# Reordering the stretch between the dense part and the experts, ending on a small pair, and summing the last tiles half in PSUM and half on VectorE

## The chip, the core and the metric

The kernel runs on one core of a Trainium2 chip. The metric is device time in microseconds (us). The engines are TensorE (PE: matmuls; PEld: its weight loads), VectorE (DVE), ScalarE (ACT), GpSimd (POOL) and SyncE (SP), which here only issues DMAs. Each engine takes its instructions in its own program order and waits on semaphores for the others. SBUF holds tiles of 128 partitions; PSUM holds what TensorE accumulates.

## What is computed

One layer of a decoder trunk over 1024 tokens of width 1024, in float32, and a final RMSNorm. Its dense part is a conditioned norm, one combined projection, a convolution branch and an mLSTM branch, and an output projection. Behind it stands a mixture of 32 experts: each token chooses one group of four and in it two of eight experts.

```python
x = x + gt1[:, None, :] * y                      # dense part
h = modulate(rmsnorm(x, g_norm2[l]), sh2, sc2)
g_sel = argmax(softmax(h @ w_rg + b_rg))         # one group of 4
top_p, top_e = top_k(softmax((h @ w_re + b_re)[group]), 2)
w_tok = p_g * top_p / sum(top_p)
y = sum over the 2 experts e of w_tok[e] * ((silu(h @ w_e_gate[e]) * (h @ w_e_up[e])) @ w_e_down[e])
x = x + gt2[:, None, :] * y
return rmsnorm(x, g_final)
```

Each expert has 3 x 2 MB of weights; all 32 are read, 192 MB.

## The kernel before, in words

Tokens lie in 8 tiles of 128 (`NT = 8`; `LT`, the last, is tile 7). The dense part ends with the output product of each tile (`products`, six or so matmuls to a k of eight), its residual (`residual`, DVE), its second norm, its router logits (`router_T` transposes, `router`) and the choice of experts (`choose`, DVE, some thirty small operations; `weigh` computes the softmax weights, in steps that the queue `fill`/`drain` hands out between other work). Tile 7 is done in two halves, so that its choice ends last. Then ranks are counted (`ranks_early`, `set_key`), and one order of experts by load is made (`places`: `elist`, `capr`, `pos`).

After that the experts run as *blocks* of 128 slots. Blocks 0 to 15 have one expert each; their weights are split on the chip into two fp32r parts, `wh` (a cast on ACT) and `wl` (a subtraction on DVE), and multiplied in three passes. Block 0's up and down weights are taken whole, in fp32 (`WHOLE`). Blocks 16 to 23 (`SMALL`) are pairs of experts with 64 slots each and take their weights as they are. Block 24 (`TWB`) shares the weights of block 2. A block goes through `st_sel` (a 0/1 matrix from positions, DVE 128x2048), `st_slots` (16 small matmuls give the slots' token numbers and weights, DVE turns them into indices, POOL gathers the rows `xg` from `h_d`), `st_x` (transpose), `st_gu` (gate and up products), `st_act`, `st_h` and `st_down` (product with the down weights; `ye` is the weighted result, scattered by POOL into `y_d`).

The table `units` sets the order of blocks and with it the order of the weight stream: 192 DMAs of 1 MB on SP into six buffers `big`, each issued when its buffer has been used up. A block's up and gate weights are asked for ahead of the down weights of the one before it. Four of the six buffers exist only once the dense part's memory is released (`yp.release()`, line 1550).

The last `LATE` blocks (two before) are not scattered. Their results are split in high and low parts (`yh`, `yl`) and put to the tokens by matmuls with the transposed 0/1 matrix (`selT`). The rest is read back: 16 loads `y_d` of 512 KB, queued on SP behind the weights (`load_y`), two for each token tile. For tiles 0 and 1 these are added to the residual `mg` by POOL or DVE, for tiles 2 to 7 one of the two is added to the other by POOL and the sum then to `mg` by DVE (tiles 2, 3) or, for tiles 4 to 7, by matmuls with the identity into the same PSUM. Then `final_norm` (ACT square with a sum, two small POOL operations) and `final_out` (DVE, then a DMA).

```python
units = [[0], [1], [16], [2, TWB], [17], [3], [4], [18], [5], [6], [19], [7], [8], [20], [9], [10], [21], [11], [12],
         [22], [13], [23], [14], [15]]
```

Of the kernel before, what the change touches and what calls it, by code (L numbers as in the profile page):

```python
# [8 lines left out]
F32 = mybir.dt.float32  # L9
# [27 lines left out]
LATE = 2  # L37
# [5 lines left out]
def hybrid_layer_kernel(ctx: ExitStack, tc: tile.TileContext, x, c, w_ada, b_ada, g_norm1, w_in, b_if,  # L43
# [1164 lines left out]
    rev = rp.tile([P, EPG], F32, name="rev")  # L1208
    t4 = [rp.tile([P, NT, NG], F32, name=f"t4{i}") for i in range(3)]
# [126 lines left out]
    def order_of_experts():  # L1336
# [17 lines left out]
        ts(tw[0:NE], ion[0:NE], rc, OP.is_equal)  # L1354
        yield 0
# [12 lines left out]
        kp = mo.tile([P, NT, NE], F32, tag="tHL", bufs=2, name="kp")  # L1368
        ts(kp, rank, float(P), OP.is_ge, float(P * (TWB - FIX - 1)), OP.mult)
        tt(kp, kp, rank, OP.add)  # L1370
# [79 lines left out]
    def add_pieces(b, wi):  # L1450
        for q in range(2):
            for r in places(b):
# [8 lines left out]
             [22], [13], [23], [14], [15]]  # L1461
# [14 lines left out]
    for t in range(NT):  # L1476
# [18 lines left out]
        if t < NT - 1:  # L1495
            for k in range(KT):
                products(k, (0, 1))
                if k == 2 and t > 0:
                    router_T(t - 1)
# [10 lines left out]
            for _ in range(6 if t < 6 else 20):  # L1510
                fill(0)
# [37 lines left out]
    sel_into(0, slice(0, LT))  # L1549
# [84 lines left out]

    identb = rp.tile([P, P], BF16, name="identb")
    V.tensor_copy(identb, ident)
# [114 lines left out]
    def st_down(unit):  # L1751
# [24 lines left out]
        for b in unit:  # L1776
# [4 lines left out]
            for hf in range(2):  # L1781
                sl = slice(hf * 512, (hf + 1) * 512)
                stt(y[:, sl], py[b][hf], d["wsl"], gt2[:, sl], OP.mult, OP.mult)
                if b == blocks[-1]:
                    split(yhl[0][:, sl], yhl[1][:, sl], y[:, sl])
            if late:
                lates.append(yhl + [y])
# [4 lines left out]
    for r in range(FIX):  # L1792
        if r:
            sel_into(r, slice(0, LT))
# [46 lines left out]
    def load_y():  # L1841

        W.room()
        bufs = [W.buffers()[i // 2][:, i % 2 * D:(i % 2 + 1) * D] for i in range(9)]
        bufs += [xgs[(len(blocks) + i) % 3] for i in range(3)]
# [225 lines left out]
```

## Time and profile before

| | |
|---|---|
| median of 3 runs | 1435.85 us (1435.72 to 1435.99) |
| the profiled execution: its own time | 1434.2 us |
| its span, from first to last instruction | 1432.4 us |
| mean granted TensorE clock | 0.963 |
| busy: PE, DVE, ACT, POOL | 1303.9, 999.9, 513.7, 326.8 us |

Four stretches are seen in the page's forty slices: the dense part to about 796 us, in which TensorE is busy; the boundary, about 796 to 870 us, in which TensorE and the DMA engines both have gaps; the stream of expert weights, whose last byte lies about 1390 us; and the end to 1432 us, with the sums and the last norm. A busy TensorE has its engine's share near 1; a full DMA system has a share near 1.0 at about 400 GB/s.

### The profile page before, as it was taken

To read this page: it belongs to the slowest core of one execution; us is meant where nothing else is said; L and a number is where in the kernel's file an instruction comes from. 1 tells how busy PE (TensorE), PEld (TensorE's weight loads), DVE (VectorE), ACT (ScalarE), POOL (GpSimd) and SP (SyncE) were. 2 spreads that over 40 slices of the span, in tenths; PEclk is the share of its full clock that TensorE was granted. 3 is DMA by queue.
4 is the path that set the end of the run, shared out by engine and by line. 5 is a ranking of instruction groups with operands and counts; after the bars stand their busy time and mean duration, and the time that the engine had idled before them with its cause. 6 is when DMAs were issued, how large, how long until landed. Compare 5 with 4: busy or idle time off the path is not lost. (4 is left out here: it accounts for less than half of the span.)

```text
span 1432.4 us, 17703 instructions
## 1 busy us (share of the span) xinstructions
PE 1303.9 (91%) x6627; PEld 973.3 (68%) x6627; DVE 999.9 (70%) x1371; ACT 513.7 (36%) x682; POOL 326.8 (23%) x265
## 2 busy tenths in 40 slices
PE   4799989999989999999999679999899999999976
PEld 3687888879878888777887445656465565654554
DVE  6979998889976761655556685457676675754587
ACT  5233143333532224411222323335344353533442
POOL 3333455231331310115222010001111111110033
PEclk9799989999999999999999899999999999999998
DMA  9433443333353433444521578899999999999982
GB/s 288 126 118 133 140 140 119 132 118 88 115 175 125 154 114 129 168 155 154 175 102 59 191 259 331 331 379 407 418 414 404 407 401 402 405 385 399 397 337 119
DMA packets 121161, 337.13 MB, mean 235 GB/s; under 512 B 12481, under 2 KB 74221, under 8 KB 96240
## 3 DMA queue, kind: packets, MB, share of 16 engines
q1 hardware_dynamic: 106064, 290.81, 54.4%
q0 software_dynamic: 14528, 43.56, 8.1%
q10 hardware_dynamic: 480, 1.59, 0.3%
q8 instruction: 53, 0.87, 0.2%
q14 instruction: 36, 0.29, 0.1%
HBM read 303.37 MB, written 41.45 MB: 241 GB/s over the span
## 5 line engine op out<-in xcount | busy, mean ns | idle before, releaser
L56 DVE TENSOR_TENSOR wl<-big,wh 128x1024 fp32r<-128x1024 f32 x184 | 224.7, 1256 | 104.5 <-ACT wh L148 103.4
L148 ACT CAST wh<-big 128x1024 fp32r<-128x1024 f32 x184 | 185.5, 1048 | 174.8 <-DMA big<-in_w_e_gate_dram 90.8
L64 DVE SCALAR_TENSOR_TENSOR cacc<-u,vec,cacc 128x1024 f32<-128x1024 f32 x120 | 212.0, 1767 | 2.9
L67 PE MATMUL z<-hH,wh 128*128 128x512 f32 x512 | 166.3, 407 | 7.4 <-DVE hH L377 5.1
L67 PE MATMUL gu<-wh,tHLx 128*128 128x512 f32 x528 | 169.3, 401 | 2.6 <-ACT wh L148 2.6
L67 PE MATMUL z<-hL,wh 128*128 128x512 f32 x512 | 163.0, 400 | 1.4 <-DVE hL L56 1.2
L67 PE MATMUL z<-hH,wl 128*128 128x512 f32 x512 | 162.2, 398 | 0.0
L67 PE MATMUL gu<-big,tFx 128*64 128x512 f32 (+1 forms) x528 | 131.8, 628 | 0.0
L67 PEld LDWEIGHTS gu<-wh,tHLx 128*128 128x128 f32 x528 | 96.7, 189 | 29.5 <-ACT wh L148 9.5
L67 PEld LDWEIGHTS z<-hH,wh 128*128 128x128 f32 x512 | 96.2, 192 | 29.3 <-ACT hH L380 5.1
L67 PEld LDWEIGHTS z<-hL,wh 128*128 128x128 f32 x512 | 97.3, 190 | 26.1 <-DVE hL L56 1.9
L67 PEld LDWEIGHTS z<-hH,wl 128*128 128x128 f32 x512 | 97.3, 190 | 23.6 <-DVE wl L56 0.2
L67 PE MATMUL gu<-wl,tHLx 128*128 128x512 f32 x264 | 106.1, 402 | 7.7 <-DVE wl L56 7.6
L1617 POOL DMA_INDIRECT y_d<-ye,idx x23 | 32.6, 1416 | 339.1 <-DVE ye L64 319.0
L56 DVE TENSOR_TENSOR wl<-raw,wh 128x1024 fp32r<-128x1024 f32 (+1 forms) x45 | 70.7, 1575 | 39.5 <-ACT wh L148 39.5
L67 PEld LDWEIGHTS gu<-big,tFx 128*64 128x64 f32 (+1 forms) x528 | 39.8, 146 | 73.7 <-issue 71.6
L56 POOL TENSOR_TENSOR acc<-acc,ar 128x1024 f32<-128x1024 f32 x24 | 70.5, 2939 | 61.5 <-ACT ar L572 51.8
L67 PE MATMUL zt<-wl,hH 128*128 128x256 f32 (+1 forms) x256 | 76.1, 297 | 4.5 <-DVE wl L56 4.5
L67 PE MATMUL zt<-wh,hH 128*128 128x256 f32 (+1 forms) x256 | 77.3, 302 | 0.8 <-ACT qk L659 0.7
L67 PE MATMUL zt<-wh,hL 128*128 128x256 f32 (+1 forms) x256 | 76.2, 298 | 0.0
L67 PE MATMUL o<-woH,mHL 128*128 128x512 f32 x256 | 72.9, 401 | 0.0
L67 PE MATMUL py<-wh,tHLh 128*128 128x512 f32 x256 | 72.5, 405 | 0.1
(403 smaller groups left out, 2193.2 us busy)
## 6 DMA issues: line engine op xcount, KB each, us to landing
big<-in_w_e_gate_dram SPq DMA_DIRECT2D x64, 1024.0 KB
big<-in_w_e_up_dram SPq DMA_DIRECT2D x64, 1024.0 KB
big<-in_w_e_down_dram SPq DMA_DIRECT2D x64, 1024.0 KB
raw<-in_w_in_dram SPq DMA_DIRECT2D x38, 512.0 KB
ar<-in_w_ada_dram SPq DMA_DIRECT2D x16, 1024.0 KB
araw<-in_w_ada_dram SPq DMA_DIRECT2D x8, 1024.0 KB
y_d<-zero SPq DMA_DIRECT2D x16, 512.0 KB
big<-y_d SPq DMA_DIRECT2D x9, 512.0 KB
```

What stands on the lines that cost most here:

```text
L56: return eng.tensor_tensor(out=o, in0=a, in1=b, op=op)
L64: return V.scalar_tensor_tensor(out=o, in0=a, scalar=s, in1=b, op0=op0, op1=op1)
L67: return PE.matmul(o, l, r, start=start, stop=stop)
L148: S.copy(h, src)
L1617: G.indirect_dma_start(out=y_d[:, :], out_offset=bass.IndirectOffsetOnAxis(ap=idx[:, 1:2], axis=0), in_=src, in_offset=None, bounds_check= ...
```

## The change

In the boundary: the weights of the choice (`drain`) are finished inside tile 6, the router of tiles 6 and 7 is put at other steps of the product, both 0/1 matrices for tokens of tiles 0 to 6 are made together, the constant `identb` is made earlier, a one-element Silu is put ahead of block 0, one weight piece is split ahead of its transposed rows, the third `xg` is cleared later, block 16's slots come behind all four up steps of block 0, and block 0's own slots behind those; block 17's slots and the overflow counts come later in the loop.

At the end: the unit order, `LATE` one instead of two (so block 14 is now scattered as well, and only block 23 is put in by `selT`), `selT` made one unit earlier, the loads of `y_d` in the order of `ENDS` into other buffers, and the sums: tiles 0 to 3 take the residual and both loads into PSUM by identity matmuls and are normed from there, tiles 4 to 7 take both loads on DVE.

```diff
-LATE = 2
+LATE = 1
+    V.tensor_copy(identb, ident)          # moved up from before by_slot
+        ts(kp, rank, float(P), OP.is_ge, float(P * (TWB - FIX - 1)), OP.mult)   # moved up in places()
+        tt(kp, kp, rank, OP.add)
-             [22], [13], [23], [14], [15]]
+             [22], [13], [14], [15], [23]]
+                if k == 1 and t == NT - 2:
+                    drain()
-            for _ in range(6 if t < 6 else 20):
+            for _ in range(6):
                 fill(0)
...
-                if k == 3:
+                if k == 2:
                     router_T(t - 1)
-            router(t - 1)
+                if k == 5:
+                    router(t - 1)
...
-                if k == KT - 1:
-                    router(t, (0,))
                 products(k, (1,))
-                if k == 3:
+                if k == 4:
                     router_T(t, (0,))
-                if k == 5:
+                if k == 6:
                     ranks_early()
...
+            router(t, (0,))
-    sel_into(0, slice(0, LT))
+    for r in range(FIX):
+        sel_into(r, slice(0, LT))
...
-    for g_ in xgs:
+    def clear_xg(g_):
         S.activation(k3(g_), iota.unsqueeze(1).broadcast_to([P, KT, P]), AF.Copy, scale=0.0)
+    for g_ in xgs[0:2]:
+        clear_xg(g_)
...
                 stt(y[:, sl], py[b][hf], d["wsl"], gt2[:, sl], OP.mult, OP.mult)
-                if b == blocks[-1]:
+                if late:
                     split(yhl[0][:, sl], yhl[1][:, sl], y[:, sl])
...
+    S.activation(mo.tile([P, 1], F32, tag="silu", bufs=1, name="silu"), pio, AF.Silu)
+    W.split()
+    clear_xg(xgs[2])
     next(places_)
     st_x(0)
-    W.split()
-    W.split()
+    next(places_)
     next(rest)
-    next(places_)
     for _ in rest:
         pass
     W.nsplit = 4
-    st_gu(0, 0, 0, 4)
     for b in blocks_of(2):
         st_sel(b)
+    st_gu(0, 0, 0, 4)
+    W.split()
     W.split()
     W.split()
     st_x(1)
-    st_gu(0, 1, 0, 2)
+    st_sel(0)
+    st_gu(0, 1, 0, 4)
     for b in blocks_of(2):
         st_slots(b)
-    st_sel(0)
-    st_gu(0, 1, 2, 4)
     st_slots(0, False)
...
+        bufs = list(xgs)                  # load_y: 3 xg, 4 whl, 4 u, 4 halves of big, 1 tHL
...
+        for t in ENDS:
             for i in range(2):
-                yin[t, i] = bufs[2 * t + i]
+                yin[t, i] = bufs.pop(0)
                 nc.sync.dma_start(yin[t, i], y_d[i * T + t * P:i * T + (t + 1) * P, :])
+    ENDS = (4, 0, 5, 1, 6, 2, 7, 3)
+    def by_ident(t, a, start):
+        for hf in range(2):
+            mm(ends[t][hf], ident, a[hf], start, False)
+    def begin_end(t):
+        ends[t] = zps.tile([P, 2, 512], F32, tag="z", name=f"yl{t}")
+        ends[t] = [ends[t][:, 0, :], ends[t][:, 1, :], ends[t]]
+        by_ident(t, [x1_of(t)[:, hf * 4:hf * 4 + 4, :] for hf in range(2)], True)
     def sum_y(t):
-        if t < 2:
+        if t < 4:
             for i in range(2):
-                into_x1(t, yin[t, i], V if t else G)
+                by_ident(t, halves(yin[t, i]), False)
         else:
-            tt(yin[t, 0], yin[t, 0], yin[t, 1], OP.add, eng=G)
+            for i in range(2):
+                into_x1(t, yin[t, i])
...
-        for b in blocks_of(i + 3) if i else []:
+        for b in blocks_of(i + 3) if i > 1 else []:
             st_slots(b)
...
+        for b in blocks_of(i + 3) if i == 1 else []:
+            st_slots(b)
...
-        fill(0)
-        fill(0)
+        if i == 4:
+            drain()
+        if nxt and not after:
+            sel = sels[blocks[-1]]
+            tt(sel[:, 0], sel[:, 0], sel[:, 1], OP.add)
+            selT = uo.tile([P, T], F32R, tag="ar", bufs=2, name="selT")
+            by_slot(selT, [sel[:, 0, t, :] for t in range(NT)])
...
         if not nxt:
-            for h_, l_, y in lates:
-                split(h_, l_, y)
-            for n in range(LATE):
-                sel = sels[blocks[len(blocks) - LATE + n]]
-                tt(sel[:, 0], sel[:, 0], sel[:, 1], OP.add)
-                by_slot(selT[:, n, :], [sel[:, 0, t, :] for t in range(NT)])
-            for t in range(4):
-                sum_y(t)
+            begin_end(1)
+            sum_y(ENDS[0])
...
+    for n in range(4):
+        b_, a_ = ENDS[2 * n:2 * n + 2]
+        ends[b_] = [mps.tile([P, 512], F32, tag="m", name=f"yl{b_}_{hf}") for hf in range(2)]
+        if n < 2:
+            sum_y(a_)
+        late_rows(b_, True)
+        if n >= 2:
+            begin_end(a_)
+            sum_y(a_)
+        late_rows(a_, False)
+        for hf in range(2):
+            o_ = x1_of(b_)[:, hf * 4:hf * 4 + 4, :]
+            tt(o_, o_, k3(ends[b_][hf]), OP.add)
+        r_ = [final_norm(b_, mo, yin[b_, 0])]
+        r_.append(final_norm(a_, mo, yin[a_, 0], ends[a_][2].rearrange("p a b -> p (a b)")))
+        S.copy(x1_of(a_), k3(ends[a_][2].rearrange("p a b -> p (a b)")))
+        if n < 3:
+            sum_y(ENDS[2 * n + 2])
+        final_out(b_, yin[b_, 0], r_[0])
+        final_out(a_, yin[a_, 0], r_[1], ends[a_][2].rearrange("p a b -> p (a b)"), S if n == 3 else None)
```


**ScalarE at the boundary.** Before, `xg` clears, the rank copy and the three exps `t`, then the rows of block 0 (`tHLx`, high parts; `tFx`, whole):

```order
L1571 ACTIVATE xg_5934<-iota 128x1024
L1571 ACTIVATE xg_5935<-iota 128x1024
L1571 ACTIVATE xg_5936<-iota 128x1024
L1576 COPY rank<-psr_5855 128x32
L1292 ACTIVATE t_4991<-t_4991 128x12
L1293 ACTIVATE t_4997<-t_4997 128x24
L1294 ACTIVATE t_5007<-t_5007 128x3
L148 CAST tHLx_6031<-tpx_0_6033 128x512
L1660 COPY tFx_6032<-tpx_0_6033 128x512
L148 CAST tHLx_6031<-tpx_1_6041 128x512
```

Now, from the same clears to the first cast of block 0's rows:

```order
L1577 ACTIVATE xg_5937<-iota 128x1024
L1577 ACTIVATE xg_5938<-iota 128x1024
L1585 COPY rank<-psr_5860 128x32
L1294 ACTIVATE t_4993<-t_4993 128x12
L1295 ACTIVATE t_4999<-t_4999 128x24
L1296 ACTIVATE t_5009<-t_5009 128x3
L1812 ACT_TABLE_LOAD
L1812 ACTIVATE silu<-pio 128x1
L148 CAST wh_6025<-big_4955 128x1024
L1577 ACTIVATE xg_5939<-iota 128x1024
L148 CAST tHLx_6040<-tpx_0_6042 128x512
```

Between the exps and the rows there are now a table load, the Silu, a weight cast and a clear.

**VectorE from block 16's 0/1 matrix to its indices.** Before (`pm`, `sel`: the matrix; `wl`: weight parts; `tHLx`: block 1's rows; `sv`, `idx`: block 16's indices):

```order
L60 TENSOR_SCALAR pm_6109<-pos 128x16
L56 TENSOR_TENSOR sel_6111<-iota,pm_6109 128x2048
L56 TENSOR_TENSOR wl_6114<-big_5891,wh_6113 128x1024
L56 TENSOR_TENSOR wl_6118<-big_5892,wh_6117 128x1024
L56 TENSOR_TENSOR tHLx_6121<-tpx_0_6122,tHLx_6121 128x512
L56 TENSOR_TENSOR tHLx_6121<-tpx_1_6129,tHLx_6121 128x512
L1222 TENSOR_REDUCE sv_6159<-sl_6142 128x3
L60 TENSOR_SCALAR idx_6161<-sv_6159 128x2
```

Now, over the same piece of work:

```order
L60 TENSOR_SCALAR pm_6081<-pos 128x16
L56 TENSOR_TENSOR sel_6083<-iota,pm_6081 128x2048
L56 TENSOR_TENSOR wl_6112<-big_5894,wh_6111 128x1024
L56 TENSOR_TENSOR wl_6116<-big_5894,wh_6115 128x1024
L56 TENSOR_TENSOR wl_6120<-big_5895,wh_6119 128x1024
L56 TENSOR_TENSOR tHLx_6123<-tpx_0_6124,tHLx_6123 128x512
L56 TENSOR_TENSOR tHLx_6123<-tpx_1_6131,tHLx_6123 128x512
L60 TENSOR_SCALAR pm_6138<-pos 128x16
L56 TENSOR_TENSOR sel_6140<-iota,pm_6138 128x2048
L1224 TENSOR_REDUCE sv_6179<-sl_6162 128x3
L60 TENSOR_SCALAR idx_6181<-sv_6179 128x2
```

One more weight subtraction and block 0's matrix now stand ahead of block 16's indices.

**VectorE at the end.** Before, from the split of block 14's result to the first sum out of PSUM (`big`: loads of `y_d`; `wl`: block 15's last weights; `ye`: block 15's result):

```order
L56 TENSOR_TENSOR yl_10284<-ye_10282,yh_10283 128x1024
L56 TENSOR_TENSOR sel_9636<-sel_9636 128x1024
L56 TENSOR_TENSOR sel_9787<-sel_9787 128x1024
L56 TENSOR_TENSOR mg<-mg,big_5891 128x8x128 x2
L56 TENSOR_TENSOR wl_10406<-big_5892,wh_10405 128x1024
L56 TENSOR_TENSOR wl_10416<-big_5892,wh_10415 128x1024
L64 SCALAR_TENSOR_TENSOR ye_10431<-py_0_10397,sv_9897,gt_5932 128x512
L56 TENSOR_TENSOR yl_10433<-ye_10431,yh_10432 128x512
L64 SCALAR_TENSOR_TENSOR ye_10431<-py_1_10398,sv_9897,gt_5932 128x512
L56 TENSOR_TENSOR yl_10433<-ye_10431,yh_10432 128x512
L1933 TENSOR_LOAD novi
```

Now, from the last weight part of block 15 (`xg`: loads of `y_d` for tile 4; the second `ye` pair is block 23's):

```order
L56 TENSOR_TENSOR wl_10316<-big_4954,wh_10315 128x1024
L64 SCALAR_TENSOR_TENSOR ye_10344<-py_0_10313,sv_9730,gt_5935 128x512
L64 SCALAR_TENSOR_TENSOR ye_10344<-py_1_10314,sv_9730,gt_5935 128x512
L56 TENSOR_TENSOR hs_10368<-gu_10246,hs_10368 128x512
L56 TENSOR_TENSOR mg<-mg,xg_5937 128x8x128
L56 TENSOR_TENSOR mg<-mg,xg_5938 128x8x128
L64 SCALAR_TENSOR_TENSOR ye_10429<-py_0_10411,sv_9914,gt_5935 128x512
L56 TENSOR_TENSOR yl_10431<-ye_10429,yh_10430 128x512
L64 SCALAR_TENSOR_TENSOR ye_10429<-py_1_10412,sv_9914,gt_5935 128x512
L56 TENSOR_TENSOR yl_10431<-ye_10429,yh_10430 128x512
L1959 TENSOR_LOAD novi
```

The subtractions are no longer between the `y_d` sums and the last result; the `0/1` sum of two halves, once two, is one and stands a unit earlier.

## Rows read from the trace of the kernel before

**Rows 1.** The page's first line.
```profile
span 1432.4 us, 17703 instructions
```

**Rows 2.** Stretches of time; columns in the second line.
```profile
core 0: us, PE busy (x) PEld busy (x) DVE busy (x) ACT busy (x) POOL busy (x), PEclk, DMA share, GB/s
800.00:830.00 30.00, 17.18 (x89) 11.72 (x89) 22.66 (x80) 10.66 (x17) 2.19 (x2) 0.73 0.29 95
830.00:870.00 40.00, 35.27 (x199) 19.80 (x197) 27.56 (x49) 11.98 (x15) 7.79 (x5) 0.90 0.75 275
...
960.00:1060.00 100.00, 93.45 (x488) 60.16 (x484) 71.16 (x80) 48.61 (x57) 13.70 (x10) 1.00 1.01 413
...
1385.00:1390.00 5.00, 4.37 (x15) 3.11 (x13) 4.97 (x3) 2.10 (x3) 3.52 (x2) 0.76 0.95 379
1390.00:1395.00 5.00, 3.54 (x13) 2.36 (x13) 3.42 (x5) 0.62 (x1) 0.00 (x0) 1.00 0.07 27
```

**Rows 3.** TensorE timeline, boundary: start, us, line, operation, count, [idle before <-releaser].
```profile
779.86 1.32 PE L1141 MATMUL x1p<-ident,mg 128*128 128x128 f32 x8 [1.61 <-DVE mg L56]
...
790.51 0.66 PE L1141 MATMUL x1p<-ident,mg 128*128 128x128 f32 x4 [1.96 <-DVE mg L56]
...
827.62 0.59 PE L67 MATMUL sl<-Vc,sel 128*128 128x9 bf16 x16 [4.23 <-DVE sel L56]
...
841.74 1.13 PE L1673 MATMUL tpx<-ident,xg 128*128 128x128 f32 x8 [1.29 <-DMA xg<-h_d,idx]
...
859.45 0.59 PE L67 MATMUL sl<-Vc,sel 128*128 128x9 bf16 x16 [2.87 <-DVE sel L56]
859.98 6.18 PE L67 MATMUL gu<-big,tFx 128*64 128x512 f32 x16
...
866.77 3.65 PE L67 MATMUL gu<-big,tFx 128*64 128x512 f32 x16
```

**Rows 4.** GpSimd timeline, gathers at the boundary.
```profile
806.21 1.19 POOL L1612 DMA_INDIRECT xg<-h_d,fidx  x1 [8.17 <-DVE sel L56]
...
832.05 2.52 POOL L1612 DMA_INDIRECT xg<-h_d,idx  x1 [23.25 <-issue]
```

**Rows 5.** VectorE timeline, boundary.
```profile
842.40 1.77 DVE L64 SCALAR_TENSOR_TENSOR nbs<-nbd,nbs 128x32 f32<-128x32 f32 x8
...
857.11 2.29 DVE L56 TENSOR_TENSOR sel<-iota,pm 128x2048 bf16<-128x2048 f32 x1
```

**Rows 6.** ScalarE timeline, boundary.
```profile
833.26 1.28 ACT L1743 ACT_TABLE_LOAD   x1 [12.60 <-PE gu L67]
```

**Rows 7.** TensorE timeline, a pair's down product and the end.
```profile
1342.06 7.09 PE L67 MATMUL py<-big,tFh 128*64 128x512 f32 x32
...
1392.27 0.62 PE L67 MATMUL py<-wl,tHLh 128*128 128x512 f32 x2
...
1396.25 0.50 PE L67 MATMUL yl<-yh,selT 128*128 128x512 f32 x1 [1.53 <-ACT yh L148]
...
1416.45 0.62 PE L67 MATMUL yl<-yl,selT 128*128 128x512 f32 x2
1416.90 1.88 PE L67 MATMUL yl<-yrs,ident 128*128 128x512 f32 x4
```

**Rows 8.** VectorE timeline, the end.
```profile
1382.88 6.71 DVE L56 TENSOR_TENSOR mg<-mg,big 128x1024 f32<-128x1024 f32 x2
...
1397.59 1.22 DVE L56 TENSOR_TENSOR mg<-mg,yl 128x1024 f32<-128x1024 f32 x1 [0.67 <-PE yl L67]
...
1405.62 2.99 DVE L56 TENSOR_TENSOR mg<-mg,big 128x1024 f32<-128x1024 f32 x1
...
1422.66 1.28 DVE L56 TENSOR_TENSOR mg<-mg,yl 128x512 f32<-128x512 f32 x2
...
1426.16 1.29 DVE L64 SCALAR_TENSOR_TENSOR yrt<-mg,r,gfr 128x1024 f32<-128x1024 f32 x1 [1.03 <-POOL r L144]
```

**Rows 9.** DMA issues: line, queue, count, median us to landing.
```profile
y_d<-ye,idx POOLq DMA_INDIRECT x23, 9.1
```

More of the change, by code (lines that the diff above doesn't have):

```diff
@@ L1208, in hybrid_layer_kernel @@
     rev = rp.tile([P, EPG], F32, name="rev")
+    identb = rp.tile([P, P], BF16, name="identb")
+    V.tensor_copy(identb, ident)
     t4 = [rp.tile([P, NT, NG], F32, name=f"t4{i}") for i in range(3)]
@@ L1354, in order_of_experts @@
         ts(tw[0:NE], ion[0:NE], rc, OP.is_equal)
+        kp = mo.tile([P, NT, NE], F32, tag="tHL", bufs=2, name="kp")
+        ts(kp, rank, float(P), OP.is_ge, float(P * (TWB - FIX - 1)), OP.mult)
+        tt(kp, kp, rank, OP.add)
         yield 0
@@ L1875, in hybrid_layer_kernel @@
             load_y()
+            begin_end(0)
         st_h(unit[-1])
@@ L1887, in hybrid_layer_kernel @@
                 st_sel(b)
[L1888 to L1900 removed]
+        if i == 4:
[5 more added lines that the diff above has]
+            by_slot(selT, [sel[:, 0, t, :] for t in range(NT)])
+            gf[0] = cvp.tile([P, D], F32, tag="s", bufs=4, name="gfr")
+            on_all_rows(gf[0], vec[:, 120:128])
+        if not nxt:
+            begin_end(1)
+            sum_y(ENDS[0])
         st_down(unit)
@@ L1927, in final_norm @@
         return r3_
-    def final_out(t, o, r3_):
-        stt(k3(o), x1_of(t), r3_, k3(gf[0]), OP.mult, OP.mult)
-        (S if t == NT - 1 else nc.sync).dma_start(out[t * P:(t + 1) * P, :], o)
-    nov = nc.values_load(novi[0:1, 0:1], min_val=0, max_val=NOVF)
-    r3 = {}
-    for t in range(NT + 1):
-        if t < NT:
-            if t % 2:
-                ps = [mps.tile([P, 512], F32, tag="m", name=f"yl{t}_{hf}") for hf in range(2)]
-            else:
-                ps_ = zps.tile([P, 2, 512], F32, tag="z", name=f"yl{t}")
-                ps = [ps_[:, hf, :] for hf in range(2)]
-            on_pe = t >= NT - 4
-            for n in range(LATE):
-                for i in range(2):
-                    for hf in range(2):
-                        mm(ps[hf], selT[:, n, t * P:(t + 1) * P], lates[n][i][:, hf * 512:(hf + 1) * 512],
-                           n == 0 and i == 0, not on_pe and n == LATE - 1 and i == 1)
-            if on_pe:
-                for hf in range(2):
-                    mm(ps[hf], ident, yin[t, 0][:, hf * 512:(hf + 1) * 512], False, True)
-            if t + 4 < NT:
-                sum_y(t + 4)
-            if t % 2:
-                for hf in range(2):
-                    o_ = x1_of(t)[:, hf * 4:hf * 4 + 4, :]
-                    tt(o_, o_, k3(ps[hf]), OP.add)
-            else:
-                into_x1(t, ps_.rearrange("p a b -> p (a b)"))
-            if 2 <= t and not on_pe:
-                into_x1(t, yin[t, 0])
-            r3[t] = final_norm(t, mo, yin[t, 1])
-        if t > 0:
-            final_out(t - 1, yin[t - 1, 1], r3[t - 1])
@@ new lines, in final_out, with late_rows @@
+    def final_out(t, o, r3_, src=None, eng=None):
+        stt(k3(o), x1_of(t) if src is None else k3(src), r3_, k3(gf[0]), OP.mult, OP.mult)
+        (eng or nc.sync).dma_start(out[t * P:(t + 1) * P, :], o)
+    def late_rows(t, first):
+        for i in range(2):
+            for hf in range(2):
+                mm(ends[t][hf], selT[:, t * P:(t + 1) * P], lates[i][:, hf * 512:(hf + 1) * 512], first and i == 0, i == 1)
+    nov = nc.values_load(novi[0:1, 0:1], min_val=0, max_val=NOVF)
+    outs = []
@@ new lines, in hybrid_layer_kernel @@
+    for n in range(4):
[8 more added lines that the diff above has]
+        late_rows(a_, False)
+        for hf in range(2):
+            o_ = x1_of(b_)[:, hf * 4:hf * 4 + 4, :]
[7 more added lines that the diff above has]
+        final_out(a_, yin[a_, 0], r_[1], ends[a_][2].rearrange("p a b -> p (a b)"), S if n == 3 else None)
```

31 lines of the change are left out of this document (10 added, 21 removed).

## The prediction

> **What bounds the kernel now.** I read the forty slices first, then the table of stretches, then each engine's timeline at the two places that the change touches. The profiled execution took 1434.2 us for a span of 1432.4 [rows 1], so 1.8 us lie around the span, and the median shown is 1.65 us above that execution: I add 3.45 us to a span to get a median.
>
> Three regimes follow one another behind the dense part. At the boundary neither TensorE nor the DMA engines are full: in 800 to 830 TensorE is busy 17.18 of 30 us and the DMA share is 0.29, in 830 to 870 the share is 0.75 [rows 2]. That is 21 and 10 us of DMA time that the weight stream does not get. The stream itself is bound by bytes: in 960 to 1060 the DMA share is 1.01 at 413 GB/s, TensorE is busy 93.45 of 100 us [rows 2]. The end is neither: the share is 0.95 in 1385 to 1390 and 0.07 in the five us behind it [rows 2], so the last `y_d` load lands at about 1390, and 42.4 us of sums and norms follow before 1432.4 [rows 1]. What ends the kernel is therefore the date of the last weight byte plus a chain behind it. The sixteen loads of 524 KB stand behind the weights in the same queue; at 0.41 MB/us they take 20.4 us, so the last weight landed near 1369.5, and the end came 62.9 us later. The change shifts the first number by its boundary part and replaces the second by its tail part.
>
> **The boundary.** TensorE waits 1.61 and 1.96 us for the transposes' input [rows 3]. DVE was held there by the finishing of the weights of the choice, which the diff's `drain` now puts ahead of tile 6's residual, into a wait of DVE. Both waits can go: 3.6 us on the first gather, issued at 806.21 before [rows 4]. Little of it reaches block 0's gate product, because the order on ScalarE now has four instructions between the exps and the casts of block 0's rows. One is the table load, 1.28 us, taken from 833.26 where it stood ahead of `hs` [rows 6]; the cast and the clear of 128x1024 I set at 1.2 us each by the nearest row of that size, DVE's 1.22 [rows 8]. That is 3.7 us on an engine that was waiting for the gather, so I keep 1 us at this point. If ScalarE was free earlier by as much, the bound is 3.6, if not it is about 0.
>
> Next, TensorE waited 4.23 us for block 16's matrix in the middle of block 0's up product [rows 3]. Now the matrix is made ahead of the gate product and the up product runs through. What follows it is new: DVE has a third weight subtraction (1.22) and block 0's matrix (2.29, the form in [rows 5]) ahead of block 16's indices, 3.5 us, and TensorE will wait about 3 us for block 0's matrix before block 1. The gain on block 16's gather (832.05 before [rows 4]) is so only 1 to 2.5 us. TensorE's wait for its landing, 1.29 us [rows 3], stays. Up to block 1's second product I count 2 us.
>
> The larger part comes one step later. Before, block 17's matrix on DVE (2.29 at 857.11 [rows 5]) holds TensorE for 2.87 us, and the sixteen matmuls behind that wait then take 6.18 us where the next sixteen of the same form take 3.65 [rows 3]: half the clock behind a gap. The change puts block 17's slots behind block 16's gate product and takes the overflow counts (1.77 and some small ones at 842.40 [rows 5]) out of DVE's queue here. The wait goes, and the slow product with it: 2.87 + 2.53 = 5.4. With the 2 us that makes 7.4; I take 7. TensorE is the engine that frees the weight buffers up to 900 us, so what it gains there the stream starts earlier. From both sides: all five waits and the slow product together are 14.5 us, of which the new wait for block 0's matrix takes 3 back, so 11 is the far end; the near end is minus 1, if the new wait of block 0's slots costs as much as the old one and the weights that now come earlier delay the gathers.
>
> **The stream.** With `LATE` one, block 14 is scattered too. One scatter moves 0.5 MB, 1.3 us of the stream at 0.41 MB/us. The new order has three large blocks in a row where it had two. A block's 6.3 MB take 15.3 us. A pair needs about 23 us of TensorE (7.09 for the down third [rows 7], twice that for gate and up, and its transposes). Two large blocks and a pair take 61 us of stream, of which TensorE is busy 93% [rows 2]: 57 us, so a large block has 17. The third in a row adds 1.7 us of lag to the 3.4 of two, and six buffers hold 15.3 us: I cost it at nothing, and at 1.7 to 6 if the lag meets a buffer that isn't free. The last weight then lands at 1369.5 - 7 + 1.3 = 1363.8.
>
> **The tail.** The pair's four down pieces come last, unsplit. Its down product is 7.09 us [rows 7], of which the part behind the last byte is some 4.2. The order on VectorE shows the two sums for tile 4 ahead of the pair's `ye`. Their loads are first in the queue (2 x 0.524 MB / 0.41 = 2.6 us); with 1.22 a sum [rows 8] DVE is free about 6.4 us behind the last weight, and this, not the product, starts `ye`. From the last down matmul at 1392.27 + 0.62 to the last wait for `yh` at 1396.25 it was 3.4 us before [rows 7]; with the low part 3.8. The split result is complete 10.2 us behind the last weight (9.2 to 11).
>
> What remains is four rounds of two tiles. A pair of `selT` matmuls takes 0.45 (1416.45 to 1416.90), a tensor added by identity 1.88 [rows 7]. After the split TensorE has: round 1, 4 pairs, 1.8; round 2, two loads and 4 pairs, 5.6; rounds 3 and 4, residual, two loads and 4 pairs, 7.4 each. Together 22.2. DVE needs 1.28 for the sum out of PSUM [rows 8], 2 x 1.22 and 2 x 1.29 a round, 6.3, so TensorE paces the last rounds. Behind its last matmul: the norm (2.2 from DVE's sum at 1422.66 + 1.28 to the last scaling at 1426.16), the scaling, 1.29, and the output DMA, from 1427.45 to 1432.4 before, 4.95 [rows 8, 1]: 8.4. In all 10.2 + 22.2 + 8.4 = 40.8; some handing over from DVE to TensorE between the rounds makes it 41.3, with 39 to 46 for both ends. The other loads of `y_d` land 5.1 to 20.5 us behind the last weight, each before its round asks for it. A scatter takes 9.1 us to land [rows 9]; block 15's is issued ahead of the pair's second product, so that it is down when the first load may start.
>
> DVE's sums of `y_d` into `mg` cost 2.99 to 3.36 us each while POOL added loads too, and 1.22 for the same size while it did not [rows 8]. No POOL sum is left in the new tail. The Trainium skill, "SBUF — State Buffer", section "Terms", says that VectorE and GpSimd share a port pair, held for a whole instruction, the loser blocked; the trace agrees (2.99 against 1.22). By that rule the eight sums and eight scalings stay at the short price.
>
> **Sum.** Span 1363.8 + 41.3 = 1405.1, plus 3.45: 1408.6, said as 1409.
>
> **Rivals.** First, the boundary gives nothing: ScalarE's four instructions and the new wait for block 0's matrix eat it, or the earlier weights delay the gathers. For it speaks that the landing of a gather already ended a wait (1.29 [rows 3]); against it that the 5.4 us at block 17 depend on neither. Then the last weight lands at 1370.8, and the time is 1416.
>
> Second, three large blocks starve the ring, or the first `y_d` load waits for block 15's scatter: 3 to 8 us more, 1412 to 1417, middle 1415. For it, PE's 93.45 of 100 us [rows 2] leave little; against it, the pair behind them gives TensorE 7.7 us back.
>
> Third, on the other side: TensorE runs the tail at its lower clock. From the pair's down product to the end it now has 7.1 + 12 x 1.88 + 16 x 0.45 = 36.9 us of work, where before DVE did most sums. At 1.2 GHz it doubles, and the time is 1409 + 37 = 1446, 0.7% slower. It decides from the point where 27 of the 37 are paid, about three quarters of the tail at half clock. For it: the granted clock was 0.76 in 1385 to 1390 [rows 2], and 6.18 against 3.65 shows what a gap leaves behind. Against it: in 1390 to 1395 it was 1.00 again, with TensorE busy 3.54 of 5 us [rows 2], and the new rounds are denser than that. The Trainium skill, "TensorE: Matmul & The Clock Gate", section "HAM oscillation — how this bites in real kernels", warns that matmul groups with DMA waits between them run each at the low clock; the loads are due before their rounds here, so by that rule it would take late loads.
>
> Fourth, the change does nothing to the time: the tail's gain only if the last sums were hidden, which 42.4 us without weights contradict.
>
> **How the numbers follow.** Forecast as worked out, 1402 to 1414: 0.58. Boundary without gain, 1416: 0.14. Starved ring or late loads, 1415: 0.12. Better than 1402 (boundary nearer its 11, a denser tail): 0.07. Tail at the lower clock for most of it: 0.05. No change: 0.04. Faster by over 0.2% is what the first four make, 0.91; within 0.2%, about what a measurement of this kernel can tell from no change, 0.04; slower 0.05. The range goes from 1401 (the boundary at 11 and the tail at 39 give 1402) to 1421 (the first two rivals together give 1422).
>
> **What would show it.** Right: TensorE's waits at the two transposes gone, no wait at block 17's slots and its first product near 3.65 us, DMA share over 0.75 in 830 to 870; the last weight near 1364, the first `yh` matmul about 10 us later, rounds of 5.6 to 7.4 us, 1.22 a sum. Wrong: gather landings later than before, a DMA share below 0.95 around the three large blocks, `selT` or identity matmuls at twice their price, or TensorE waiting for `y_d` in the last rounds.

## The result, and the profile after

The changed kernel takes 1417.59 us (median of 4 runs, 1411.8 to 1424.42) against 1435.92 for the kernel before (4 runs, 1435.72 to 1436.04): ratio 0.9874, 95% interval 0.983 to 0.9919. That is 18.3 us faster where 27 were forecast, inside the range of 1401 to 1421. The profiled execution is the shortest of the four, 1411.8 us with a span of 1410.1; it is set beside the sum of the prediction (span 1405.1) below, and lies 5.8 us under the median.

The spread is not the changed kernel's alone. On the chip of the first experiments the kernel before spread from 1429.13 to 1438.71 (13 runs, median 1433.3). So every version below is set against the kernel before on the same chip, by their ratio, and versions run on different chips are compared by these ratios.

The stretches of the changed kernel, in the columns of [rows 2], and behind them two of the kernel before, which [rows 2] doesn't have:

```profile
core 0: us, PE busy (x) PEld busy (x) DVE busy (x) ACT busy (x) POOL busy (x), PEclk, DMA share, GB/s
800.00:830.00 30.00, 22.86 (x118) 15.91 (x119) 23.89 (x70) 11.77 (x19) 3.26 (x3) 0.74 0.41 140
830.00:870.00 40.00, 39.60 (x227) 23.18 (x227) 27.78 (x35) 11.49 (x15) 7.81 (x5) 1.00 0.88 340
960.00:1060.00 100.00, 93.74 (x484) 59.98 (x482) 70.06 (x81) 45.31 (x55) 12.00 (x9) 1.00 1.01 415
1300.00:1340.00 40.00, 40.00 (x188) 29.65 (x188) 31.58 (x33) 25.39 (x30) 8.08 (x3) 1.00 0.98 400
1340.00:1360.00 20.00, 17.65 (x86) 10.42 (x82) 5.93 (x7) 4.20 (x6) 0.98 (x1) 0.91 0.88 329
1360.00:1380.00 20.00, 20.00 (x71) 8.80 (x70) 9.58 (x11) 5.47 (x9) 1.75 (x2) 1.00 1.02 411
1385.00:1390.00 5.00, 5.00 (x16) 2.62 (x15) 3.43 (x4) 2.68 (x5) 3.66 (x4) 1.00 0.38 154
```

```profile
1300.00:1340.00 40.00, 36.00 (x165) 18.89 (x165) 20.31 (x23) 14.40 (x18) 3.74 (x3) 1.00 0.99 397
1340.00:1360.00 20.00, 19.44 (x89) 11.61 (x88) 12.66 (x14) 10.88 (x13) 1.70 (x1) 1.00 1.00 389
```

In 800 to 830 the DMA share is 0.41 instead of 0.29, in 830 to 870 it is 0.88 instead of 0.75, with the clock at 1.00 instead of 0.90 [rows 2]. The stream from 960 on is as before. New is 1300 to 1360: TensorE is busy 40.00 of the first 40 us instead of 36.00, and in 1340 to 1360 the DMA share falls to 0.88, where it was 1.00. The last `y_d` load lands about 1387 (0.38 of five us behind 1385) instead of 1390.

TensorE at the boundary:

```profile
776.81 1.32 PE L1141 MATMUL x1p<-ident,mg 128*128 128x128 f32 x8 [1.30 <-DVE mg L56]
...
786.76 0.66 PE L1141 MATMUL x1p<-ident,mg 128*128 128x128 f32 x4
...
792.42 0.66 PE L1141 MATMUL x1p<-ident,mg 128*128 128x128 f32 x4 [1.43 <-DVE mg L56]
...
807.71 1.94 PE L1663 MATMUL tpx<-ident,xg 128*128 128x128 f32 x8 [2.67 <-ACT wh L148]
...
819.21 7.03 PE L67 MATMUL gu<-big,tFx 128*128 128x512 f32 x16
...
827.51 0.56 PE L67 MATMUL sl<-Vc,sel 128*128 128x9 bf16 x16 [0.89 <-DVE sel L56]
...
834.25 1.14 PE L1679 MATMUL tpx<-ident,xg 128*128 128x128 f32 x8
...
849.01 3.65 PE L67 MATMUL gu<-big,tFx 128*64 128x512 f32 x16
...
858.27 0.47 PE L67 MATMUL py<-wh,tHLh 128*128 128x512 f32 x1
```

Of the two waits at the transposes [rows 3] that of 1.61 us is still there, 1.30, and that of 1.96 is gone (786.76). The last transposes of the dense part, at 792.42, wait 1.43 us; before, they stood at 796.31 and waited 0.78. The wait of 4.23 us for block 16's matrix and the split up product are gone: sixteen matmuls run through in 7.03. Block 0's slots wait 0.89 us, block 16's rows not at all, and at 849.01 the first product of block 16 takes 3.65 us where it took 6.18 [rows 3]. Block 1's down product starts at 858.27, 13 us earlier than the 871.27 of before.

GpSimd's gathers, which answer to [rows 4], and on VectorE block 16's matrix, which stood at 825.26 before:

```profile
803.01 1.13 POOL L1621 DMA_INDIRECT xg<-h_d,fidx  x1 [8.86 <-DVE ord L56]
...
828.48 0.99 POOL L1621 DMA_INDIRECT xg<-h_d,idx  x1 [22.90 <-ACT wh L148]
```

```profile
818.15 2.29 DVE L56 TENSOR_TENSOR sel<-iota,pm 128x2048 bf16<-128x2048 f32 x1
```

TensorE, VectorE and GpSimd at the end:

```profile
1343.44 0.62 PE L1648 MATMUL selT<-identb,sel 128*128 128x128 bf16 x8 [2.35 <-DVE sel L56]
1343.90 3.05 PE L67 MATMUL row<-ident,vec 128*128 128x128 f32 x16
1346.60 1.83 PE L67 MATMUL py<-wh,tHLh 128*128 128x512 f32 x4
...
1383.46 1.98 PE L67 MATMUL yl<-mg,ident 128*128 128x512 f32 x4 [0.58 <-DVE xg L64]
...
1396.86 0.63 PE L67 MATMUL yl<-yl,selT 128*128 128x512 f32 x2
```

```profile
1373.96 0.69 DVE L56 TENSOR_TENSOR yl<-ye,yh 128x512 fp32r<-128x512 f32 x1 [0.68 <-ACT yh L148]
...
1376.80 2.48 DVE L56 TENSOR_TENSOR mg<-mg,yrw 128x1024 f32<-128x1024 f32 x2
...
1398.71 1.27 DVE L56 TENSOR_TENSOR mg<-mg,yl 128x512 f32<-128x512 f32 x2
1402.21 1.28 DVE L64 SCALAR_TENSOR_TENSOR big<-mg,r,gfr 128x1024 f32<-128x1024 f32 x1 [2.23 <-ACT big L1945]
1404.27 1.28 DVE L64 SCALAR_TENSOR_TENSOR big<-yl,r,gfr 128x1024 f32<-128x1024 f32 x1 [0.77 <-POOL r L144]
```

```profile
1378.16 1.21 POOL L60 TENSOR_SCALAR r<-r 128x1 f32<-128x1 f32 x1 [22.58 <-ACT xg L1945]
...
1401.30 0.22 POOL L60 TENSOR_SCALAR r<-r 128x1 f32<-128x1 f32 x1 [3.83 <-ACT big L1945]
...
1402.30 1.27 POOL L60 TENSOR_SCALAR r<-r 128x1 f32<-128x1 f32 x1
```

TensorE waits 2.35 us for the 0/1 sum, which VectorE does behind three weight parts of block 15, then does the row and the first matmuls of block 15's down product at a lower pace (3.05 and 1.83 us; further on four such matmuls take 1.10; the granted clock is 0.83 in 1340 to 1350), and from there to 1397.5 it has work without a gap but for 0.58 and 0.42 us. The split result is complete at 1373.96 + 0.69. Two sums of `y_d` take 2.48 us on VectorE, 1.24 each, where the forecast had 1.22; no sum of GpSimd stands beside them, as forecast. Behind TensorE's last matmul (1396.86 + 0.62) 6.8 us pass to the last scaling and 12.6 to the end of the span.

### The profile page after: what moved, and what is told of

Its sections match the earlier page's. It is cut to its first block, busy times and chain, and to the rows that moved or that the text cites. A ratio compares the mean times of both kernels' runs of the same rounds, so it can differ in the third digit from the quotient of the medians.

```text
span 1410.1 us, 17680 instructions
## 1 busy us (share of the span) xinstructions
PE 1301.6 (92%) x6619; PEld 973.0 (69%) x6619; DVE 985.6 (70%) x1369; ACT 515.0 (37%) x685; POOL 318.4 (23%) x258
## 5 line engine op out<-in xcount | busy, mean ns | idle before, releaser
L67 PE MATMUL gu<-big,tFx 128*64 128x512 f32 (+1 forms) x528 | 128.9, 625 | 0.0
L1626 POOL DMA_INDIRECT y_d<-ye,idx x24 | 37.7, 1571 | 327.1 <-DVE ye L64 309.9
```

The lines of the kernel that those rows point to most:

```text
L67: return PE.matmul(o, l, r, start=start, stop=stop)
L1626: G.indirect_dma_start(out=y_d[:, :], out_offset=bass.IndirectOffsetOnAxis(ap=idx[:, 1:2], axis=0), in_=src, in_offset=None, bounds_check= ...
```

## The experiments

**The changed kernel again.** No edit.

> The changed kernel once more, unchanged, for the spread of its times (1411.8 to 1424.4 in four runs, where before spread over 0.3 us). Theory A: the spread is TensorE at its lower clock on a path that TensorE now bounds; taking the two clock levels, the time at the lower one is 2 x (1 - mean clock) x span, 90 us at span 1410.1 and 114 us at 1422.7, and each further us of it costs half a us. Then new runs lie on the same line (span = 1410 + 0.5 x (low-clock time - 90), within 2 us). Rival: the spread comes from DMA landings (gathers, y_d loads), and span and mean clock do not go together.

Measured: 1415.13 us (4 runs, 1413.74 to 1419.4), ratio 0.9877 (0.9847 to 0.9908) beside 1433.3. By span and clock the four were 1413.1 at 0.966, 1412.0 at 0.971, 1413.7 at 0.967 and 1417.7 at 0.967. The line puts them at 1413, 1406, 1412 and 1412: two fit, two lie 6 us above it. Theory A falls as the whole cause. In the first four runs the low clock went with the time, but the kernel before spreads as much with clocks of 0.960 to 0.968, and what makes an execution longer stays open. The traces tell where it does. In the six of them whose end holds the same work of TensorE (the changed kernel three times, the last round's order twice, the two splits put back) it is 115.2 to 115.9 us from block 22's down product to the last matmul, but 446.6 to 450.7 from block 0's down product to block 22's: the end hardly spreads, the stream does.

**The boundary part alone.**

```diff
 LATE = 2                                      # and the unit order, load_y, sum_y and the end as before
+        for b in blocks_of(i + 3) if i == 1 else []:     # the boundary's edits all in place
+            st_slots(b)
```

> Only the boundary part (unit order, LATE, sums and loads at the end as before). Theory A: from 900 to 1360 us the stream is bound by bytes, so the 12 us that the boundary gained in the profiled execution arrive whole at the end: 1435.9 - 12 = 1424, with a spread under 1 us because the stream hides dips of the clock. Rival: what the boundary gains is lost again in the stream, 1430 or more.

Measured: 1425.54 us (10 runs), ratio 0.9943 (0.992 to 0.9966), 8.2 us under before on that chip, 4.9 to 11.5 by the interval. In its trace block 1's down product is 14.0 us earlier than in the trace of before (857.29), and the last `y_d` load is issued 12.9 us earlier (1369.15 instead of 1382.02): what is gained at 870 us is there at 1369. Its stream stays full to the end:

```profile
1300.00:1340.00 40.00, 37.01 (x162) 19.41 (x158) 19.30 (x21) 16.01 (x19) 1.17 (x2) 1.00 1.00 398
1340.00:1360.00 20.00, 19.16 (x83) 14.93 (x83) 18.28 (x19) 14.08 (x17) 1.52 (x1) 1.00 1.00 411
```

In 1300 to 1360 the DMA share is 1.00 where the changed kernel has 0.98 and 0.88. So the boundary's gain arrives, by the medians 8 us, by the two traces 13. Theory A had 12, which lies just outside the interval of the medians, and a spread under 1 us; the ten runs spread over 12.8.

**The end and the unit order alone.**

```diff
+LATE = 1                                      # order, loads and sums as changed
-        for b in blocks_of(i + 3) if i == 1 else []:     # the boundary as before
```

> Only the unit order and the new end, boundary as before. Theory A (both parts add, the end is bound by TensorE from the three large blocks on): the changed kernel's end, 12 us later: about 1424 in the best run, up to 1436 in one with many dips, median about 1429. Rival (the lost gain at the end is due to the earlier stream, so that a later stream finds a TensorE that has caught up): 1418 to 1421, because the end loses nothing in its three large blocks.

Measured: 1422.4 us (4 runs), ratio 0.9925 (0.9896 to 0.9953), 10.7 us under before (6.7 to 14.9). That is between the two expectations; taken as differences from before (7 and some 16 us) neither is excluded at its near end. The parts add: 8.2 + 10.7 = 18.9, the whole 17.6 on the same chip. The new end is so worth about 11 us by the medians, where the sum had 20. By the traces it is more: from block 22's down product to the end of the span it was 140.8 us before, is 126.5 here and 128.3 in the changed kernel.

**Three large blocks earlier.**

```diff
-             [21], [11], [12], [22], [13], [14], [15], [23]]
+             [21], [11], [12], [13], [22], [14], [15], [23]]
```

> The changed kernel with block 13 ahead of block 22, so that the three large blocks in a row are 11, 12, 13, and two (14, 15) stand ahead of the last pair. Theory A (three large blocks make TensorE late when the last pair's weights wait for buffers): the DMA share of 0.78 and 0.60 near 1335 and 1355 us rises to 0.95 and more, the time falls by 3 to 6 us. Rival (TensorE is late because of the wait for the 0/1 sum and the selT transposes ahead of block 15's down product): the time stays within 1 us of the changed kernel's.

Measured: 1414.29 us, ratio 0.9871 (0.9839 to 0.9904), the changed kernel's beside it 0.9877. The stream does lose less:

```profile
1300.00:1340.00 40.00, 39.44 (x183) 26.19 (x181) 25.30 (x26) 20.07 (x24) 4.68 (x3) 1.00 1.00 406
1340.00:1360.00 20.00, 16.79 (x90) 9.49 (x90) 7.51 (x8) 6.69 (x8) 0.97 (x1) 1.00 0.96 370
```

The share is 1.00 and 0.96 instead of 0.98 and 0.88, and the time is within 1 us of the changed kernel's 1415.13 on this chip. The intervals would hide some 4 us; as far as they tell, the three in a row are not what costs the end its gain, and the DMA gap is not what decides.

**The 0/1 sum and selT earlier.**

```diff
-        if nxt and not after:                  # sum, selT, row: behind the gate product
+        if nxt and not after:                  # ahead of it
             sel = sels[blocks[-1]]
         if nxt:
             ws = st_gu(nxt[0], 0, 0, 2)
```

> The changed kernel with block 23's 0/1 sum, its selT transposes and the final norm's row ahead of block 23's gate product instead of behind it. Theory A (TensorE is late at the end because these stand ahead of block 15's down product: an idle 2.35 us, then 3.05 us of row at the low clock; so the last pair's buffers come free late and the DMA share falls to 0.16 to 0.6 around 1354 to 1359): the idle gap ahead of selT goes, the DMA gap shrinks, and the last y_d load and the end come 3 to 5 us earlier. Rival (TensorE is late from the sum of its work in the last 100 us, whatever the order): at most 2 us.

Measured: 1417.85 us (5 runs), ratio 0.9867 (0.9841 to 0.9894): no gain that can be told from the changed kernel's 0.9877. The edit did not remove the wait and made a larger DMA gap:

```profile
1344.00:1350.00 6.00, 6.00 (x30) 3.36 (x30) 0.00 (x0) 1.36 (x3) 0.00 (x0) 0.85 0.04 16
```

```profile
1342.20 0.95 PE L1648 MATMUL selT<-identb,sel 128*128 128x128 bf16 x8 [2.01 <-DVE sel L56]
...
1379.42 1.99 PE L67 MATMUL yl<-xg,ident 128*128 128x512 f32 x4 [0.64 <-DMA xg<-y_d]
```

TensorE still waits 2.01 us for the sum and six us go with a DMA share of 0.04, and yet no difference in the times can be told, at intervals of some 4 us to either side. Theory A falls. In the trace the hole costs TensorE one wait for data, 0.64 us for the first `y_d` load. So a hole of six us in the stream, this near to the end, shows in the trace with less than one us of waiting: the stream hardly bounds there.

**The last round in another order.**

```diff
+            ra_ = final_norm(a_, mo, yin[a_, 0], end_a)      # the last round: the PSUM tile first
+            rb_ = final_norm(b_, mo, yin[b_, 0])
+            final_out(a_, yin[a_, 0], ra_, end_a)
+            final_out(b_, yin[b_, 0], rb_, None, S)
```

> The changed kernel with, in the last round alone, the tile whose sum stays in PSUM normed and written first and the other last. Theory A (behind TensorE's last matmul 6.8 us pass to the last scaling instead of the 2.2 that I had, because the norm of the tile that DVE sums comes first on ScalarE and the two follow one another): 0.8 to 2 us earlier from the last matmul to the end. Rival (GpSimd's small operations, which take 1.2 to 1.3 us instead of 0.22 beside VectorE, set the pace): within 0.5 us.

Measured: 1411.65 us (5 runs), ratio 0.9814 (0.9788 to 0.9841). More than either theory said, and so run again beside the changed kernel (below).

**Both moves.** The two edits above together.

> The two edits together (0/1 sum and selT early; last round's order). If each acts on its own stretch, the end comes earlier by the sum of the two: 4 to 7 us by theory A of each, under 2.5 us by their rivals.

Measured: 1417.98 us (4 runs), ratio 0.9873 (0.9846 to 0.99). That is 0.6 us better than the changed kernel by the ratios, so the sum of the rivals (under 2.5), not that of the theories. In its trace the last round's gain is there all the same: from the last matmul (1405.41) to the end (span 1415.9) it is 10.5 us, as with the last round's edit alone. That this edit alone was 6.3 us faster beside it on the same chip can't come from that stretch, and stays open.

**The boundary without its steps in the loop.**

```diff
-        for b in blocks_of(i + 3) if i == 1 else []:     # block 17's slots and the overflow counts as before
-            st_slots(b)
+        fill(0)
+        fill(0)
```

> Only the boundary part, without its steps in the expert loop: block 17's slots and the overflow counts stay where they were. In the trace the boundary gained 7.5 us up to block 0's down product and 5.2 more at block 17's. Theory A (the second is the 2.87 us wait plus the product at half clock): the wait and the 6.2 us product are back, block 1's down product comes 5 us later than with the whole boundary part, and the time lies half-way between before and the whole part. Rival (with the earlier boundary the wait for block 17's matrix would be gone anyway): the same as the whole part.

Measured: 1430.47 us (12 runs), ratio 0.9966 (0.9949 to 0.9983): 4.9 us under before, the whole part 8.2. TensorE in its trace, block 17's slots and block 16's gate product:

```profile
850.83 0.56 PE L67 MATMUL sl<-Vc,sel 128*128 128x9 bf16 x16 [2.87 <-DVE sel L56]
851.31 5.35 PE L67 MATMUL gu<-big,tFx 128*64 128x512 f32 x16
```

The wait of 2.87 us is back and so is a slow product (5.35 us, 6.18 before), and block 1's down product starts 4.5 us later than with the whole part (861.78 and 857.29). In the trace theory A holds. The times fit it, half-way between before and the whole part, but they come from two chips and their intervals overlap.

**The last round, on one chip with the changed kernel.** The changed kernel for measure:

> The changed kernel unchanged, on the same chip as the next three, as their measure. 1412 to 1422 us, median about 1416, by the ratio of 0.9877 that it had beside before.

Measured: 1416.2 us (5 runs, 1412.9 to 1422.13), ratio 0.9888 (0.9868 to 0.9908). And the last round's edit:

> The last round's order swapped, once more beside the changed kernel on one chip. By the traces 1.8 us lie between the two from TensorE's last matmul to the end (10.8 instead of 12.6): theory A, 1.5 to 2.5 us below the median of the changed kernel. Rival: the 0.6% lower ratio of the first run was all due to the swap, 6 us or more.

Measured: 1414.65 us (4 runs, 1411.54 to 1415.89), ratio 0.9858 (0.9843 to 0.9873). VectorE, GpSimd and TensorE at its end:

```profile
1404.91 1.27 DVE L56 TENSOR_TENSOR mg<-mg,yl 128x512 f32<-128x512 f32 x2
1406.11 1.28 DVE L64 SCALAR_TENSOR_TENSOR big<-yl,r,gfr 128x1024 f32<-128x1024 f32 x1
1408.41 1.28 DVE L64 SCALAR_TENSOR_TENSOR big<-mg,r,gfr 128x1024 f32<-128x1024 f32 x1 [1.03 <-POOL r L144]
```

```profile
1407.51 0.22 POOL L60 TENSOR_SCALAR r<-r 128x1 f32<-128x1 f32 x1 [1.64 <-ACT big L1945]
```

```profile
1403.09 0.62 PE L67 MATMUL yl<-yl,selT 128*128 128x512 f32 x2
```

From the last matmul (1403.71) to the end (span 1414.2) it is 10.5 us, 2.1 less than the changed kernel's 12.6, and 1.6 between the medians: theory A's size, though the intervals of the two overlap. The 2.1 us have two parts. ScalarE is done with both norms 3.7 us behind the last matmul instead of 4.7, since it no longer takes one behind the other at the last moment. And GpSimd's second addition takes 0.22 us (1407.51) instead of 1.27 (1402.30 in the changed kernel), because no scaling of VectorE runs beside it now. So half of the gain is what theory A named, and half is what its rival in the first run of this edit named. By the ratios this version lies under the changed kernel in both runs, by 1.6 us beside it here and by more in the first, where the two were not run together.

**Less work for TensorE.** This version leaves the residual of tiles 0 and 1 out of the sum.

```diff
-        by_ident(t, [x1_of(t)[:, hf * 4:hf * 4 + 4, :] for hf in range(2)], True)
+        if t >= 2:
+            by_ident(t, [x1_of(t)[:, hf * 4:hf * 4 + 4, :] for hf in range(2)], True)
```

> The changed kernel without the identity products that put the residual of tiles 0 and 1 into PSUM (that part of the sum is left out), 3.8 us of TensorE's work ahead of the pair's down product. Theory A (from the three large blocks on, the end is TensorE's own work, one instruction behind the other): 3 to 4 us earlier. Rival (the end is set by the last weight and the y_d loads, as I had predicted): within 1 us.

Measured: 1410.45 us (5 runs, 1409.25 to 1413.35), ratio 0.9843 (0.983 to 0.9857): 5.8 us under the changed kernel's median, 3.7 between the two traces (1407.4 and 1411.1). TensorE ahead of the pair's down product, first here, then in the changed kernel on the same chip:

```profile
1344.08 2.00 PE L67 MATMUL row<-ident,vec 128*128 128x128 f32 x16
...
1351.60 7.09 PE L67 MATMUL gu<-big,tFx 128*64 128x512 f32 x32
1360.13 0.75 PE L1679 MATMUL tph<-ident,hs 128*128 128x128 f32 x4 [1.45 <-DVE hs L56]
1361.56 7.09 PE L67 MATMUL py<-big,tFh 128*64 128x512 f32 x32 [0.68 <-ACT tFh L1680]
```

```profile
1344.98 3.54 PE L67 MATMUL row<-ident,vec 128*128 128x128 f32 x16
...
1354.04 7.09 PE L67 MATMUL gu<-big,tFx 128*64 128x512 f32 x32
...
1365.16 7.09 PE L67 MATMUL py<-big,tFh 128*64 128x512 f32 x32
```

The product starts at 1361.56 instead of 1365.16, and everything behind it comes 3.6 us earlier. But 0.8 us of this is there already when `selT` starts (1343.62 instead of 1344.43), and 1.6 comes from `selT` and the row, which run ahead of the matmuls left out: the row's sixteen matmuls take 2.00 us here and 3.54 there, with a granted clock in 1340 to 1350 of 1.00 and 0.83. From the pair's gate product to its down product it is 9.96 instead of 11.12 us: 1.2 us are the edit's. Most of the rest of the 3.8 us goes into two new waits, 1.45 and 0.68, for the pair's activations and not for a weight. So theory A has its direction in the trace, at a third of its size: TensorE's work paces this stretch, but the activations follow 1.2 us behind. Why the medians lie 5.8 us apart is not shown.

**Two splits back ahead of the ranking.**

```diff
     st_x(0)
+    W.split()
+    W.split()
     next(places_)
```

> The changed kernel with two of the weight splits of block 0 issued again ahead of the ranking of experts (as before), instead of behind block 16's 0/1 matrix. Theory A (block 16's matrix came 7 us earlier in VectorE's queue because the splits, which wait for ScalarE's casts, no longer stand ahead of the ranking): the matrix ends 3 to 5 us later, block 0's up product ends before it all the same, block 16's and 0's slots wait 2 to 4 us more, and block 0's down product comes 2 to 4 us later. Rival (the early finish comes from the earlier choice and the order of the first gathers): within 1 us.

Measured: 1414.62 us (4 runs), ratio 0.9859 (0.9844 to 0.9875), not later than the changed kernel's 0.9888. Its trace (an execution of 1421.6 us) does show what theory A says:

```profile
802.14 0.18 PE L67 MATMUL psr<-oab,strib 128*128 128x32 bf16 x1 [4.36 <-DVE oab L56]
...
831.61 0.59 PE L67 MATMUL sl<-Vc,sel 128*128 128x9 bf16 x16 [2.88 <-DVE sel L56]
...
841.65 7.03 PE L67 MATMUL py<-big,tFh 128*128 128x512 f32 x16
```

From the last ranks (802.14 here, 799.69 in the changed kernel) to block 16's matrix it is 22.4 us instead of 18.5, block 0's slots wait 2.88 instead of 0.89, and to block 0's down product it is 39.5 instead of 35.5. The 4 us are in the trace and not in the times. Between executions that spread over 9 us such a step is at the edge of what four runs show. Theory A is so seen in one trace and not confirmed by the time.

## Why the prediction was right, and where it was not

**Direction and range** were right: both parts gain, 8.2 and 10.7 us each alone, and the slower case did not come. The gain was 18 us instead of 27. The clock is 1.00 in 1360 to 1390 and TensorE's rounds there are dense, as I had argued against that rival.

**The first waits.** The step "both waits can go" was half right: the one of 1.96 us went, with its transposes two steps later in the product, the one of 1.61 fell to 1.30, and the last transposes wait 0.65 us more than before. The gather is 3.2 us earlier all the same; 2.7 of them stand already ahead of the first wait. What gave them is not shown, and part is the execution: the last ranks come at 802.6 and 803.6 us in the two traces without the boundary's edits, at 798.1 to 803.3 in the twelve with them.

**ScalarE's four instructions.** Right: block 0's rows are transposed from 807.71 and the up product starts only 0.6 us earlier than before (819.21 against 819.79). In this trace the transposes wait for ScalarE, 2.67 us.

**Block 16's matrix.** The step "up to block 1's second product I count 2 us" was mis-sized: 7.5 us up to block 0's down product in this trace (835.22 instead of 842.71), and 3 to 9 in the ten other traces with the same order up to there (834.1 to 839.5). I had the matrix on VectorE where it stood before. But the two weight subtractions, which wait for ScalarE's casts, no longer stand ahead of the ranking, and the matrix is made at 818.15 instead of 825.26. Of these 7.1 us 3.9 are the earlier choice (last ranks at 799.69 instead of 803.58) and 3.2 the order: from the ranks to the matrix it was 21.7 us before, is 18.5 now, and 22.4 with the splits put back.

**Block 17.** Right in mechanism and size: 5.4 forecast; in the traces the 7.5 us have become 13.0 behind it, so 5.5, and the run without it gives back the wait, a slow product and 4.5 us.

**The stream.** That the boundary's gain is carried through is right for the boundary alone. In the changed kernel's trace block 22's down product is 9.9 us earlier than before (1281.79 instead of 1291.65), not 13.0. The step that failed is the date of the last weight, "1369.5 - 7 + 1.3". By the same rule (20.4 us ahead of the last load) it is 1366.5, though the boundary gave 6 us more in this trace than I took: 8.7 us late, of which 3.1 were lost by block 22 already. For the rest I looked for the cause at the ring and at three large blocks. The traces show another: from 1296 us to its last matmul TensorE stands still for 2.35, 0.58 and 0.42 us alone, each time for VectorE and never for a weight; the pair's last buffers come free when it has used them (the DMA queue's two waits for the pair's gate product are 11.9 us), and the DMA gaps follow from that. The runs agree, as far as they go: moving the large blocks filled the gap without a change of time that can be told, making it larger cost one wait of 0.64 us, and taking 3.8 us of matmuls away gave 1.2, until the activations set the pace. How the 5.6 us divide stays open. I had summed TensorE's work for the slower rival alone (36.9 us) and not set it against the time that was left for it.

**The tail.** The split result is complete 8.2 us behind the last weight (10.2 forecast). I had VectorE's sums for tile 4 start `ye`, 6.4 us behind that weight; they were done after 3.7 (1367.62 + 2.58), and the product, 0.2 us later, started it. The rest is 35.5 instead of 31.1 us: "behind its last matmul 8.4" is 12.6. I took one norm; the last round has two, one behind the other on ScalarE and on GpSimd, and the one whose sum is ready first is behind the other; and I took GpSimd's additions at their price without VectorE beside them. Turning the norms round gave 2.1 us back in the trace, half of it from either.

The four differences, -6 at the boundary, +8.7, -2 and +4.4, make the 5.0 us between the forecast span and the measured one. The rest to 1417.6 is the distance of the median from the profiled execution.

**The rivals.** The second came near its time (1412 to 1417 against 1417.6) and in one sign, the DMA share of 0.88; the first `y_d` load waited 1.0 us for block 15's scatter (6.1 with selT early). But its mechanism is not what the traces show: the end cost more than the sum by TensorE's work and the two norms, not by a starved ring. It stands close behind, though: VectorE's sums of the first loads ended 0.2 us ahead of the product here, and some 0.5 and 1.4 us after it with less work for TensorE and with selT early. The others did not come.

## What to carry to other kernels

When a change shortens the idle stretch at one end and the chain at the other, add up what the next engine has to do in the time that remains: here TensorE was busy 93% beside a full stream, and moving sums from VectorE to it, ahead of and behind the last weights, left it with 1.0 us of pauses between 1343.4 us and its last matmul at 1397.5. A hole in the DMA share proves nothing by itself; make it larger or fill it, and see whether the end moves and which engine waits. When a version ends earlier, follow both traces back to the edit: of 3.6 us, 2.4 were there ahead of the first matmul that was left out. And before several us are put down to an edit, run the kernel before often enough on the same chip: it spread by 9.6 us here, and a single pair of traces said 13 us where ten runs said 8.

## What the runs showed of the hardware that was not expected

GpSimd's addition on 128x1 takes 0.22 us when VectorE is idle (at 1401.30) and 1.16 to 1.32 us beside it, seven times in this trace, each ending 0.1 us behind VectorE's instruction. The one at 1378.16 ends at 1379.37, when VectorE's two sums of 128x1024 end (1376.80 + 2.48 = 1379.28). The Trainium skill, "SBUF — State Buffer", section "Terms", has the port pair of the two engines held for a whole instruction, with the loser blocked; this agrees, and it shows the other side of it: not only do GpSimd's large sums slow VectorE, VectorE's also delay one element per partition on GpSimd, by what is left of their own length.

The clock behind a wait differs between executions of the same instructions: behind 2.17 us without work the row's sixteen matmuls took 2.00 us in one trace (granted clock 1.00 in 1340 to 1350) and 3.54 in another (0.83). What decides it, no run here shows.
